# A causal convolution of matrices on one core: how the node seeds in PSUM are built, and how the stream sums are grouped

## The chip, the core and the metric

The kernel runs on one core of a Trainium2 chip. The metric is the device time of one execution in microseconds. A core has five queues that matter here: TensorE (PE in the profile; PEld are its weight loads), VectorE (DVE), ScalarE (ACT), GpSimd (POOL, which only issues loads here) and SyncE (SP, which issues stores and transposes). [...]

## The reference

`x` has shape 8 x 4096 x 512, `kernel` 8 x 512 x 512, both fp32.

```python
out = np.zeros_like(x)
for k in range(8):
    shifted = x if k == 0 else np.concatenate([zeros(B, k, D), x[:, :-k, :]], axis=1)
    out += np.matmul(shifted, kernel[k])
```

Each output row is the sum over eight matrices of the row k steps earlier times matrix k.

## The kernel before, in words

The 32768 rows are spread over 128 partitions, 256 consecutive time steps on each, and are worked through in 32 iterations of eight time steps. The eight taps are halved three times (the index letters a, b, c, each LO, HI or MID), in the manner of Karatsuba: where a plain split needs four half-size products, sums and differences of the inputs ("streams") and of the matrices leave three. So 27 products remain for an iteration in place of 64. The matrices `W[a, b, c]` are built once, ahead of the loop (lines 157 to 172), by VectorE and ScalarE, in bf16.

An iteration has three nodes, a = MID, LO and HI in this order. A node makes nine products, each of four matmuls of 128x128 by 128x512 (`product`, line 179), that is 36 matmuls a node and 108 an iteration. In the notation of the code (lines 197 to 231):

- `node_u` makes product u into bank 1 of a PSUM pair `q`; ScalarE copies it to bank 0 (line 202).
- `node_a` adds one product to each bank of q; ScalarE copies the whole pair to SBUF as `ts` (1024 elements a partition, line 209).
- `node_v`, called for b = LO and HI, makes product v into bank 1 of a pair `p`; VectorE then writes both banks of p as v + ts (LO) or v - ts (HI) in one instruction of 1024 elements, which the profile lists as pp<-pp,ts (line 215, recorded under the helper's line 79).
- `node_l` adds the last product to one bank of p; two for each p.
- `node_e` empties p: ScalarE copies it to `ms` in the MID node (line 226), VectorE adds or subtracts ms in the other two, giving y, which SP stores (lines 229 to 231).

All four pairs of banks come from one pool of four (line 54); q and p share it.

The streams are tiles in SBUF in bf16, made by VectorE from XT, which holds the eight transposed input rows: D1, D2, D21 for the MID node, D4, D41, D42, D421 for LO and HI (lines 106 to 138; all recorded under line 79, and listed as D<-XT or D<-D). A single row is 512 elements a partition. XT is filled by two transposing DMAs an iteration on SP's queue (`transpose_x`, line 100), from tiles that POOL's queue loads two iterations ahead.

The schedule is written out by hand (`manual_schedule`), and every engine works in program order. The loop of lines 239 to 272 runs over nodes; while it finishes `cur`, it begins `nxt` and makes u of the node after that. One node's order is: l and l of the first p, e of the first p, a and a of nxt with ts, first stream sums, v of nxt with its pp, twice, second stream sums, l of the second p, u of the node after next, l of the second p, e of the second p. In a LO node the first stream sums are D1, D2 and the lower half of D4, the second ones the upper half of D421, which the HI node's l products read.

Of the kernel before, what the change touches and what calls it, by code (L numbers as in the profile page):

```python
# [19 lines left out]
LO, HI, MID = 0, 1, 2  # L20
# [3 lines left out]
def kernel(  # L24
# [6 lines left out]
    nc = tc.nc  # L31
    B, S, D = x.shape
    K = kernel.shape[0]
    P = 128
# [6 lines left out]
    f32 = mybir.dt.float32  # L41
    ADD = mybir.AluOpType.add
    SUB = mybir.AluOpType.subtract
    MUL = mybir.AluOpType.mult
    PSUM = bass.MemoryType.PSUM
# [5 lines left out]
    wpool = ctx.enter_context(tc.tile_pool(name="w", bufs=1))  # L51
    spool = ctx.enter_context(tc.tile_pool(name="s", bufs=1))
    xpool = ctx.enter_context(tc.tile_pool(name="x", bufs=2))
    ppool = ctx.enter_context(tc.tile_pool(name="p", bufs=4, space=PSUM))

    ctx.enter_context(tc.manual_schedule())

# [5 lines left out]
    W = {}  # L63
# [5 lines left out]
    XT = spool.tile([P, K, D], bf, name="XT")  # L69
    D4 = spool.tile([P, K, D], bf, name="D4")  # L70
    D42 = spool.tile([P, K, D], bf, name="D42")
    D421 = spool.tile([P, K, D], bf, name="D421")
    D41 = spool.tile([P, 4, D], bf, name="D41")
    D2 = spool.tile([P, 5, D], bf, name="D2")
    D21 = spool.tile([P, 4, D], bf, name="D21")
    D1 = spool.tile([P, 2, D], bf, name="D1")

    def tt(o, a, b, op):
        nc.vector.tensor_tensor(out=o, in0=a, in1=b, op=op)  # L79


    for _ in range(4):
        pw = ppool.tile([P, 2, D], f32, name="pp")
        for h in range(2):
            nc.tensor.matmul(pw[:, h], lhsT=ident, rhs=zero, start=True, stop=True)  # L85


    def load_x(i, h):
        xin = xpool.tile([P, 4, D], bf, name="xin")
        if i >= 0:  # L90
            nc.gpsimd.dma_start(out=xin, in_=xr[:, K * i + 4 * h:K * i + 4 * h + 4, :])  # L91
        else:
            nc.vector.memset(xin, 0.0)  # L93
            for b in range(B):
                nc.gpsimd.dma_start(  # L95
                    out=xin[b * G + 1:(b + 1) * G],
                    in_=xr[b * G:(b + 1) * G - 1, RUN - 8 + 4 * h:RUN - 4 + 4 * h, :])
        return xin

    def transpose_x(xin, h):  # L100
        nc.sync.dma_start_transpose(
            out=XT[:, 4 * h:4 * h + 4, :].rearrange("p j (c m) -> p (j c) m", m=P),
            in_=xin.rearrange("p j d -> p (j d)"))


    def prep_m():
        tt(D1[:, 0], XT[:, 7], XT[:, 0], SUB)
        tt(D1[:, 1], XT[:, 0], XT[:, 1], SUB)
        tt(D2[:, 0:2], XT[:, 6:8], XT[:, 0:2], ADD)
        tt(D2[:, 2:4], XT[:, 0:2], XT[:, 2:4], ADD)  # L110

    def prep_d27():
        tt(D2[:, 4], XT[:, 5], XT[:, 7], ADD)

    def prep_d21():
        tt(D21[:, 0], D2[:, 4], D2[:, 0], SUB)
        tt(D21[:, 1:4], D2[:, 0:3], D2[:, 1:4], SUB)

    def prep_d4(h):
        a, b = (XT[:, 4:8], XT[:, 0:4]) if h == LO else (XT[:, 0:4], XT[:, 4:8])  # L120
        tt(D4[:, 4 * h:4 * h + 4], a, b, ADD)

    def prep_d41_d42(h):
        if h == LO:
            tt(D41[:, 0], D4[:, 7], D4[:, 0], SUB)
            tt(D41[:, 1], D4[:, 0], D4[:, 1], SUB)
            tt(D42[:, 0:2], D4[:, 6:8], D4[:, 0:2], ADD)
            tt(D42[:, 2:4], D4[:, 0:2], D4[:, 2:4], ADD)
        else:
            tt(D41[:, 2:4], D4[:, 3:5], D4[:, 4:6], SUB)  # L130
            tt(D42[:, 4:8], D4[:, 2:6], D4[:, 4:8], ADD)

    def prep_d421(h):
        if h == LO:
            tt(D421[:, 0], D42[:, 7], D42[:, 0], SUB)
            tt(D421[:, 1:4], D42[:, 0:3], D42[:, 1:4], SUB)
        else:
            tt(D421[:, 4:8], D42[:, 3:7], D42[:, 4:8], SUB)

# [3 lines left out]
        transpose_x(xi[h], h)  # L143
    tt(D4[:, 5:8], XT[:, 1:4], XT[:, 5:8], ADD)
    tt(D42[:, 7], D4[:, 5], D4[:, 7], ADD)
    tt(D2[:, 4], XT[:, 5], XT[:, 7], ADD)
    xi = [load_x(0, 0), load_x(0, 1)]
    transpose_x(xi[0], 0)
    prep_m()
    prep_d4(LO)  # L150
    prep_d21()
    prep_d41_d42(LO)
    transpose_x(xi[1], 1)
    prep_d4(HI)
    xi = [load_x(1, 0), load_x(1, 1)]
# [19 lines left out]
    cpool = ctx.enter_context(tc.tile_pool(name="c", bufs=2))  # L175
# [3 lines left out]
    def product(bank, comp, w, start):  # L179
        for c in range(DC):  # L180
            nc.tensor.matmul(bank, lhsT=comp[:, c * P:(c + 1) * P], rhs=w[:, c, :],  # L181
                             start=start and c == 0, stop=c == DC - 1,
                             skip_group_check=True)
# [4 lines left out]
    def streams(a):  # L188

        if a == MID:  # L190
            return (XT[:, 0], [D1[:, 0], D1[:, 1]], [D2[:, 0], D2[:, 2]],
                    [D21[:, j] for j in range(4)])
        o = 4 * a
        return (D4[:, o], [D41[:, 2 * a], D41[:, 2 * a + 1]], [D42[:, o], D42[:, o + 2]],
                [D421[:, o + j] for j in range(4)])

    def node_u(i, a):
        n = Node()
        n.i, n.a, n.s = i, a, streams(a)
        n.q = ppool.tile([P, 2, D], f32, name="pp")  # L200
        product(n.q[:, 1], n.s[0], W[a, MID, MID], True)
        nc.scalar.copy(out=n.q[:, 0], in_=n.q[:, 1])  # L202
        return n

    def node_a(n):
        product(n.q[:, 0], n.s[1][0], W[n.a, MID, LO], False)
        product(n.q[:, 1], n.s[1][1], W[n.a, MID, HI], False)
        n.ts = cpool.tile([P, 2, D], f32, name="ts")
        nc.scalar.copy(out=n.ts, in_=n.q)  # L209
        n.p = {}  # L210

    def node_v(n, b_):
        n.p[b_] = p = ppool.tile([P, 2, D], f32, name="pp")
        product(p[:, 1], n.s[2][b_], W[n.a, b_, MID], True)
        tt(p, p[:, 1:2].to_broadcast([P, 2, D]), n.ts, ADD if b_ == LO else SUB)

    ms = {}

    def node_l(n, b_, j):
        product(n.p[b_][:, j], n.s[3][2 * b_ + j], W[n.a, b_, j], False)  # L220

    def node_e(n, b_):
        p = n.p[b_]
        if n.a == MID:
            ms[b_] = mpool.tile([P, 2, D], f32, name="ms")
            nc.scalar.copy(out=ms[b_], in_=p)  # L226
        else:
            y = ypool.tile([P, 2, D], f32, name="y")
            tt(y, p, ms[b_], ADD if n.a == LO else SUB)
            t0 = K * n.i + 4 * n.a + 2 * b_  # L230
            nc.sync.dma_start(out=orr[:, t0:t0 + 2, :], in_=y)

    order = [(i, a) for i in range(NIT) for a in (MID, LO, HI)]
    nodes = [node_u(*order[0])]
    node_a(nodes[0])
    node_v(nodes[0], 0)
    node_v(nodes[0], 1)
    nodes.append(node_u(*order[1]))
    for k, (i, a) in enumerate(order):
        cur = nodes[k]  # L240
        nxt = nodes[k + 1] if k + 1 < len(order) else None
        last = i + 1 == NIT
        if a == MID and not last:
            transpose_x(xi[0], 0)
        node_l(cur, 0, LO)
        node_l(cur, 0, HI)
        node_e(cur, 0)
        if nxt:
            node_a(nxt)
        if a == MID:  # L250
            prep_d421(LO)
        elif not last and a == LO:
            prep_m()
            prep_d4(LO)
        elif not last:
            prep_d21()
            prep_d41_d42(LO)
        if nxt:
            node_v(nxt, 0)
            node_v(nxt, 1)  # L260
        if a == MID:
            prep_d41_d42(HI)
            prep_d27()
        elif a == LO:
            prep_d421(HI)
        elif not last:
            prep_d4(HI)
        node_l(cur, 1, LO)
        if k + 2 < len(order):
            nodes.append(node_u(*order[k + 2]))  # L270
        node_l(cur, 1, HI)
        node_e(cur, 1)
        if a == LO and not last:
            transpose_x(xi[1], 1)
            if i + 2 < NIT:
                xi = [load_x(i + 2, 0), load_x(i + 2, 1)]
# [30 lines left out]
```

## Time and profile before

| | us |
|---|---|
| median of 3 runs | 925.17 |
| lowest, highest | 924.97, 925.95 |
| the profiled execution | 924.67 |
| its span, first to last instruction | 922.9 |
| TensorE busy (3464 matmuls) | 758.2 |
| VectorE busy | 793.2 |
| ScalarE busy | 255.9 |
| GpSimd busy | 43.0 |

The span is what the profile shows of an execution; the rest of the execution's own time lies around it. Busy time is the union of an engine's instructions. Matmuls are pipelined, so a matmul's record is longer than the distance to the next one. The first 112 us of the span hold the input's first transposes and the building of the matrices; the loop fills the rest.

### The profile page before, as it was taken

The numbers are of one execution on the slowest core, as the hardware profiler recorded it, in microseconds if no ns is written. First come the engines' busy times: TensorE is split into PE (matmuls) and PEld (weight loads), VectorE is DVE, ScalarE is ACT, GpSimd is POOL, SyncE is SP. The second block draws the span as 40 slices with busy tenths as digits, with TensorE's granted clock in tenths as the row PEclk, the third lists the DMA queues.
The fourth block names the chain that finished last, engine by engine and source line by source line (L and its number), as shares of the span: only waits on it lengthen the run. The fifth ranks groups of instructions, "written<-read, shape, count | busy, mean of one in ns | idle before, by whom it ended". The sixth has DMA issues, their size and how long they took to land.

```text
span 922.9 us, 9305 instructions
## 1 busy us (share of the span) xinstructions
PE 758.2 (82%) x3464; PEld 336.7 (36%) x3464; DVE 793.2 (86%) x954; ACT 255.9 (28%) x329; POOL 43.0 (5%) x86
## 2 busy tenths in 40 slices
PE   1000199999999999999999999999999999999997
PEld 0000044444444444444444444444444444444443
DVE  0358679999999999999999999999999999999996
ACT  0046622222222222222222222222222222222222
POOL 4000000000000000000000000000000000000000
PEclk9999999999999999999999999999999999999999
DMA  7853317867787767677776676767677876676642
GB/s 95 116 202 130 91 40 165 181 153 174 178 173 172 158 163 179 153 161 165 182 173 157 173 180 166 155 166 177 143 172 165 181 167 166 171 182 165 155 136 114
DMA packets 169709, 145.25 MB, mean 157 GB/s; under 512 B 140752, under 2 KB 140752, under 8 KB 169664
## 3 DMA queue, kind: packets, MB, share of 16 engines
q1 hardware_dynamic: 159936, 110.12, 44.0%
q0 software_dynamic: 9728, 34.54, 23.7%
q8 instruction: 27, 0.44, 0.2%
q14 instruction: 18, 0.15, 0.1%
HBM read 77.46 MB, written 67.11 MB: 157 GB/s over the span
## 4 chain that ended last, share of the span: by engine, by line
PE 61%; DVE 21%; issue 5%; ACT 0%; DVEq 0%
PE pp L181 61%; DVE D L79 11%; DVE pp L79 7%; DVE y L79 4%; ACT ts L209 0%; DVEq L79 0%; ACT w L172 0%; ACT pp L202 0%
## 5 line engine op out<-in xcount | busy, mean ns | idle before, releaser
L181 PE MATMUL pp<-w,D 128*128 128x512 bf16 x3328 | 730.5, 380 | 61.9 <-DVE D L79 53.2
L181 PEld LDWEIGHTS <-D 128*128 128x128 bf16 x3328 | 323.2, 98 | 479.0 <-DVE D L79 69.0
L79 DVE TENSOR_TENSOR pp<-pp,ts 128x1024 f32<-128x1024 f32 x192 | 226.5, 1225 | 26.2 <-ACT ts L209 26.2
L79 DVE TENSOR_TENSOR D<-D 128x512 bf16<-128x512 bf16 (+3 forms) x353 | 239.5, 731 | 0.0
L79 DVE TENSOR_TENSOR y<-pp,ms 128x1024 f32<-128x1024 f32 x128 | 156.3, 1221 | 46.4 <-PE pp L181 46.4
L79 DVE TENSOR_TENSOR D<-XT 128x512 bf16<-128x512 bf16 (+3 forms) x226 | 152.5, 722 | 34.0 <-DMA XT<-xin 34.0
L209 ACT COPY ts<-pp 128x1024 f32<-128x1024 f32 x96 | 97.2, 1013 | 276.3 <-PE pp L181 272.8
L202 ACT COPY pp<-pp 128x512 f32<-128x512 f32 x96 | 54.7, 570 | 236.4 <-PE pp L181 236.4
L181 PE MATMUL pp<-w,XT 128*128 128x512 bf16 x128 | 34.2, 385 | 96.2 <-DVE w L79 96.2
L226 ACT COPY ms<-pp 128x1024 f32<-128x1024 f32 x64 | 64.9, 1014 | 69.5 <-PE pp L181 69.5
L91 POOL DMA_DIRECT2D xin<-in_x_dram x64 | 34.0, 531 | 827.9 <-DMA XT<-xin 827.9
L181 PEld LDWEIGHTS <-XT 128*128 128x128 bf16 x128 | 12.5, 98 | 98.5 <-issue 83.8
L79 DVE TENSOR_TENSOR mid<-wt 128x1024 f32<-128x1024 f32 (+1 forms) x12 | 18.9, 1576 | 17.2 <-DMA wt<-in_kernel_dram 17.2
L171 ACT CAST w<-mid 128x512 bf16<-128x512 f32 x20 | 12.1, 605 | 71.8 <-DVE mid L79 71.8
L79 DVE TENSOR_TENSOR w<-mid 128x512 bf16<-128x512 f32 x20 | 13.1, 689 | 0.4
L172 ACT ACTIVATE w<-mid 128x512 bf16<-128x512 f32 x20 | 12.5, 625 | 0.0
L79 DVE TENSOR_TENSOR w<-wt 128x512 bf16<-128x512 f32 x16 | 10.3, 684 | 0.0
L172 ACT ACTIVATE w<-wt 128x512 bf16<-128x512 f32 x16 | 10.0, 625 | 0.0
L171 ACT CAST w<-wt 128x512 bf16<-128x512 f32 x16 | 9.6, 602 | 0.0
L95 POOL DMA_DIRECT2D xin<-in_x_dram x16 | 8.3, 530 | 1.2 <-DVE xin L93 1.2
L79 DVE TENSOR_TENSOR mid<-mid 128x1024 f32<-128x1024 f32 x4 | 4.9, 1225 | 0.3
L85 PE MATMUL pp<-zero,ident 128*128 128x512 bf16 x8 | 3.6, 630 | 1.4 <-POOL ident masks.py:199 1.4
(10 smaller groups left out, 5.3 us busy)
## 6 DMA issues: line engine op xcount, KB each, us to landing
out_dram<-y SPq DMA_DIRECT2D x128, 512.0 KB, 3.0
xin<-in_x_dram POOLq DMA_DIRECT2D x64, 512.0 KB, 5.4
wt<-in_kernel_dram SPq DMA_DIRECT2D x8, 1024.0 KB, 4.8
XT<-xin SPq DMA_TRANSPOSE x66, 5.0
xin<-in_x_dram POOLq DMA_DIRECT2D x16, 60.0 KB, 2.6
```

What stands on the lines that cost most here:

```text
L79: nc.vector.tensor_tensor(out=o, in0=a, in1=b, op=op)
L85: nc.tensor.matmul(pw[:, h], lhsT=ident, rhs=zero, start=True, stop=True)
L91: nc.gpsimd.dma_start(out=xin, in_=xr[:, K * i + 4 * h:K * i + 4 * h + 4, :])
L95: nc.gpsimd.dma_start(out=xin[b * G + 1:(b + 1) * G], in_=xr[b * G:(b + 1) * G - 1, RUN - 8 + 4 * h:RUN - 4 + 4 * h, :])
L171: nc.scalar.copy(out=W[a, b_, LO][:, c], in_=V[:, 1])
L172: nc.scalar.mul(out=W[a, b_, HI][:, c], in_=V[:, 0], mul=-1.0)
L181: nc.tensor.matmul(bank, lhsT=comp[:, c * P:(c + 1) * P], rhs=w[:, c, :], start=start and c == 0, stop=c == DC - 1, skip_group_check=True)
L202: nc.scalar.copy(out=n.q[:, 0], in_=n.q[:, 1])
L209: nc.scalar.copy(out=n.ts, in_=n.q)
L226: nc.scalar.copy(out=ms[b_], in_=p)
```

## The change

Three things change together.

1. The seed of a node. a1 (the a product of bank 1) now comes first, into bank 1 of q; ScalarE writes its negative to bank 0. Then a0 is added to bank 0 and u to bank 1. So bank 1 holds u + a1 and bank 0 holds a0 - a1. ScalarE copies bank 1 into bank 1 of the first p, its negative into bank 1 of the second p (the seeds), and bank 0 to SBUF as `dts` (512 elements). Product v is added onto the seed in bank 1, and VectorE writes bank 0 alone, as bank 1 plus or minus dts (512 elements in place of 1024). The results are the same.
2. The pools and the order. p has three pairs of banks and q one of its own. a0 and u of nxt and the first l of the second p stand ahead of the seeds; the second l of the second p, and a1 of the node after next, behind v. D421(HI) moves ahead of v in the LO node, D4(LO) behind it; D41(HI) moves ahead of v in MID.
3. The sums. D2 is stored in another order of rows, and pairs of sums are merged into one instruction, in part through operands whose row stride is negative (`XT[:, 7::-7]` is rows 7 and 0) or larger than one.

```diff
-    ppool = ctx.enter_context(tc.tile_pool(name="p", bufs=4, space=PSUM))
+    ppool = ctx.enter_context(tc.tile_pool(name="p", bufs=3, space=PSUM))
+    qpool = ctx.enter_context(tc.tile_pool(name="q", bufs=1, space=PSUM))
...
+    def pairs(z):
+        return z.rearrange("p (a b) d -> p a (b d)", b=2)
+
     def prep_m():
-        tt(D1[:, 0], XT[:, 7], XT[:, 0], SUB)
-        tt(D1[:, 1], XT[:, 0], XT[:, 1], SUB)
-        tt(D2[:, 0:2], XT[:, 6:8], XT[:, 0:2], ADD)
-        tt(D2[:, 2:4], XT[:, 0:2], XT[:, 2:4], ADD)
+        tt(D1[:, 0:2], XT[:, 7::-7], XT[:, 0:2], SUB)
+        tt(pairs(D2[:, 1:5]), pairs(XT)[:, 3::-3], pairs(XT)[:, 0:2], ADD)
...
     def prep_d21():
-        tt(D21[:, 0], D2[:, 4], D2[:, 0], SUB)
-        tt(D21[:, 1:4], D2[:, 0:3], D2[:, 1:4], SUB)
+        tt(D21[:, 0:4], D2[:, 0:4], D2[:, 1:5], SUB)
...
-            tt(D41[:, 0], D4[:, 7], D4[:, 0], SUB)
-            tt(D41[:, 1], D4[:, 0], D4[:, 1], SUB)
-            tt(D42[:, 0:2], D4[:, 6:8], D4[:, 0:2], ADD)
-            tt(D42[:, 2:4], D4[:, 0:2], D4[:, 2:4], ADD)
+            tt(D41[:, 0:2], D4[:, 7::-7], D4[:, 0:2], SUB)
...
+            tt(pairs(D42)[:, 0:2], pairs(D4)[:, 3::-3], pairs(D4)[:, 0:2], ADD)
...
-            tt(D421[:, 0], D42[:, 7], D42[:, 0], SUB)
-            tt(D421[:, 1:4], D42[:, 0:3], D42[:, 1:4], SUB)
+            tt(D421[:, 0:4:2], D42[:, 7:0:-6], D42[:, 0:4:2], SUB)
+            tt(D421[:, 1:4:2], D42[:, 0:4:2], D42[:, 1:4:2], SUB)
...
-        n.q = ppool.tile([P, 2, D], f32, name="pp")
-        product(n.q[:, 1], n.s[0], W[a, MID, MID], True)
-        nc.scalar.copy(out=n.q[:, 0], in_=n.q[:, 1])
+        n.q = qpool.tile([P, 2, D], f32, name="qq")
+        product(n.q[:, 1], n.s[1][1], W[a, MID, HI], True)
+        nc.scalar.mul(out=n.q[:, 0], in_=n.q[:, 1], mul=-1.0)
...
+    def node_a0u(n):
         product(n.q[:, 0], n.s[1][0], W[n.a, MID, LO], False)
-        product(n.q[:, 1], n.s[1][1], W[n.a, MID, HI], False)
-        n.ts = cpool.tile([P, 2, D], f32, name="ts")
-        nc.scalar.copy(out=n.ts, in_=n.q)
+        product(n.q[:, 1], n.s[0], W[n.a, MID, MID], False)
+
+    def node_seed(n):
+        for b_ in range(2):
+            n.p[b_] = ppool.tile([P, 2, D], f32, name="pp")
+            if b_ == LO:
+                nc.scalar.copy(out=n.p[b_][:, 1], in_=n.q[:, 1])
+            else:
+                nc.scalar.mul(out=n.p[b_][:, 1], in_=n.q[:, 1], mul=-1.0)
+        n.dts = cpool.tile([P, D], f32, name="dts")
+        nc.scalar.copy(out=n.dts, in_=n.q[:, 0])

     def node_v(n, b_):
-        n.p[b_] = p = ppool.tile([P, 2, D], f32, name="pp")
-        product(p[:, 1], n.s[2][b_], W[n.a, b_, MID], True)
-        tt(p, p[:, 1:2].to_broadcast([P, 2, D]), n.ts, ADD if b_ == LO else SUB)
+        p = n.p[b_]
+        product(p[:, 1], n.s[2][b_], W[n.a, b_, MID], False)
+        tt(p[:, 0], p[:, 1], n.dts, ADD if b_ == LO else SUB)
...
         node_l(cur, 0, LO)
         node_l(cur, 0, HI)
+        if nxt:
+            node_a0u(nxt)
+        node_l(cur, 1, LO)
         node_e(cur, 0)
         if nxt:
-            node_a(nxt)
+            node_seed(nxt)
         if a == MID:
             prep_d421(LO)
-        elif not last and a == LO:
-            prep_m()
-            prep_d4(LO)
+            prep_d41(HI)
+        elif a == LO:
+            if not last:
+                prep_m()
+            prep_d421(HI)
         elif not last:
+            prep_d41(LO)
+            prep_d42(LO)
             prep_d21()
-            prep_d41_d42(LO)
         if nxt:
             node_v(nxt, 0)
             node_v(nxt, 1)
         if a == MID:
-            prep_d41_d42(HI)
+            prep_d42(HI)
             prep_d27()
-        elif a == LO:
-            prep_d421(HI)
         elif not last:
-            prep_d4(HI)
-        node_l(cur, 1, LO)
+            prep_d4(LO if a == LO else HI)
+        node_l(cur, 1, HI)
         if k + 2 < len(order):
-            nodes.append(node_u(*order[k + 2]))
-        node_l(cur, 1, HI)
+            nodes.append(node_a1(*order[k + 2]))
         node_e(cur, 1)
```

## Rows read from the trace of the kernel before

**Rows 1.** The page: busy us (share) of the engines; granted TensorE clock in 40 slices.

```profile
PE 758.2 (82%) x3464; PEld 336.7 (36%) x3464; DVE 793.2 (86%) x954; ACT 255.9 (28%) x329; POOL 43.0 (5%) x86
...
PEclk9999999999999999999999999999999999999999
```

**Rows 2.** The waits: engine and line, waited for, us in total, times, longest.

```profile
PE pp L181 <- DVE D L79: 53.2, 32, 1.7
```

**Rows 3.** Windows: one iteration; us, busy us of each engine, clock, DMA share, GB/s.

```profile
424.66:449.82 25.16, 23.48 (x109) 10.47 (x108) 23.21 (x28) 6.78 (x8) 1.06 (x2) 1.00 0.71 168
```

**Rows 4.** The timeline, a LO node into a HI node: start, us, instruction, idle before.

```profile
405.64 3.09 DVE L79 TENSOR_TENSOR D<-XT 128x512 bf16<-128x512 bf16 x5
...
408.62 1.03 PE L181 MATMUL pp<-w,XT 128*128 128x512 bf16 x4
...
408.65 2.35 DVE L79 TENSOR_TENSOR pp<-pp,ts 128x1024 f32<-128x1024 f32 x2
...
409.73 0.57 ACT L202 COPY pp<-pp 128x512 f32<-128x512 f32 x1 [2.50 <-PE pp L181]
410.91 1.21 DVE L79 TENSOR_TENSOR D<-D 128x2048 bf16<-128x2048 bf16 x1
412.05 1.22 DVE L79 TENSOR_TENSOR y<-pp,ms 128x1024 f32<-128x1024 f32 x1
...
412.18 21.76 PE L181 MATMUL pp<-w,D 128*128 128x512 bf16 x100 [1.68 <-DVE D L79]
413.72 3.24 SPq L101 DMA_TRANSPOSE XT<-xin  x1
```

**Rows 5.** Groups of instructions by shape: count, busy us, mean ns, idle before.

```profile
L79 DVE TENSOR_TENSOR pp<-pp,ts 128x1024 f32<-128x1024 f32 x192 | 226.5, 1225 | 26.2 <-ACT ts L209 26.2
...
L209 ACT COPY ts<-pp 128x1024 f32<-128x1024 f32 x96 | 97.2, 1013 | 276.3 <-PE pp L181 272.8 <-issue 3.5
L79 DVE TENSOR_TENSOR D<-D 128x2048 bf16<-128x2048 bf16 x64 | 77.8, 1216 | 0.0
...
L79 DVE TENSOR_TENSOR D<-D 128x1024 bf16<-128x1024 bf16 x96 | 63.0, 683 | 0.0
L79 DVE TENSOR_TENSOR D<-D 128x1536 bf16<-128x1536 bf16 x64 | 60.9, 951 | 0.0
L202 ACT COPY pp<-pp 128x512 f32<-128x512 f32 x96 | 54.7, 570 | 236.4 <-PE pp L181 236.4
L79 DVE TENSOR_TENSOR D<-D 128x512 bf16<-128x512 bf16 x129 | 51.1, 417 | 0.0
...
L79 DVE TENSOR_TENSOR w<-wt 128x512 bf16<-128x512 f32 x16 | 10.3, 684 | 0.0
L172 ACT ACTIVATE w<-wt 128x512 bf16<-128x512 f32 x16 | 10.0, 625 | 0.0
...
L171 ACT CAST w<-wt 128x512 bf16<-128x512 f32 x16 | 9.6, 602 | 0.0
L79 DVE TENSOR_TENSOR mid<-wt 128x2048 f32<-128x2048 f32 x4 | 9.2, 2292 | 17.2 <-DMA wt<-in_kernel_dram 17.2
```

**Rows 6.** The timeline at the loop's start: the first node's products.

```profile
111.58 0.57 ACT L202 COPY pp<-pp 128x512 f32<-128x512 f32 x1
112.21 6.39 PE L181 MATMUL pp<-w,D 128*128 128x512 bf16 x22 [8.67 <-ACT pp L202]
...
114.72 0.15 PEld L181 LDWEIGHTS <-D 128*128 128x128 bf16 x1 [0.28 <-issue]
115.15 3.17 PEld L181 LDWEIGHTS <-D 128*128 128x128 bf16 x15 [0.27 <-issue]
```

**Rows 7.** DMA issues: queue, operation, count, median us to landing.

```profile
XT<-xin SPq DMA_TRANSPOSE x66, 5.0
```

More of the change, by code (lines that the diff above doesn't have):

```diff
@@ L79, in tt @@
         nc.vector.tensor_tensor(out=o, in0=a, in1=b, op=op)
-    for _ in range(4):
-        pw = ppool.tile([P, 2, D], f32, name="pp")
+    for k in range(4):
+        pw = ppool.tile([P, 2, D], f32, name="pp") if k else qpool.tile([P, 2, D], f32, name="qq")
         for h in range(2):
@@ L103, in transpose_x @@
             in_=xin.rearrange("p j d -> p (j d)"))
+    def pairs(z):
+        return z.rearrange("p (a b) d -> p a (b d)", b=2)
     def prep_m():
-        tt(D1[:, 0], XT[:, 7], XT[:, 0], SUB)
-        tt(D1[:, 1], XT[:, 0], XT[:, 1], SUB)
-        tt(D2[:, 0:2], XT[:, 6:8], XT[:, 0:2], ADD)
-        tt(D2[:, 2:4], XT[:, 0:2], XT[:, 2:4], ADD)
+        tt(D1[:, 0:2], XT[:, 7::-7], XT[:, 0:2], SUB)
+        tt(pairs(D2[:, 1:5]), pairs(XT)[:, 3::-3], pairs(XT)[:, 0:2], ADD)
     def prep_d27():
-        tt(D2[:, 4], XT[:, 5], XT[:, 7], ADD)
+        tt(D2[:, 0], XT[:, 5], XT[:, 7], ADD)
     def prep_d21():
-        tt(D21[:, 0], D2[:, 4], D2[:, 0], SUB)
-        tt(D21[:, 1:4], D2[:, 0:3], D2[:, 1:4], SUB)
+        tt(D21[:, 0:4], D2[:, 0:4], D2[:, 1:5], SUB)
     def prep_d4(h):
@@ L121, in prep_d4, with prep_d41, prep_d42 @@
         tt(D4[:, 4 * h:4 * h + 4], a, b, ADD)
-    def prep_d41_d42(h):
+    def prep_d41(h):
         if h == LO:
-            tt(D41[:, 0], D4[:, 7], D4[:, 0], SUB)
-            tt(D41[:, 1], D4[:, 0], D4[:, 1], SUB)
-            tt(D42[:, 0:2], D4[:, 6:8], D4[:, 0:2], ADD)
-            tt(D42[:, 2:4], D4[:, 0:2], D4[:, 2:4], ADD)
+            tt(D41[:, 0:2], D4[:, 7::-7], D4[:, 0:2], SUB)
         else:
             tt(D41[:, 2:4], D4[:, 3:5], D4[:, 4:6], SUB)
+    def prep_d42(h):
+        if h == LO:
+            tt(pairs(D42)[:, 0:2], pairs(D4)[:, 3::-3], pairs(D4)[:, 0:2], ADD)
+        else:
             tt(D42[:, 4:8], D4[:, 2:6], D4[:, 4:8], ADD)
@@ L145 @@
     tt(D42[:, 7], D4[:, 5], D4[:, 7], ADD)
-    tt(D2[:, 4], XT[:, 5], XT[:, 7], ADD)
+    prep_d27()
     xi = [load_x(0, 0), load_x(0, 1)]
@@ L190, in streams @@
         if a == MID:
-            return (XT[:, 0], [D1[:, 0], D1[:, 1]], [D2[:, 0], D2[:, 2]],
+            return (XT[:, 0], [D1[:, 0], D1[:, 1]], [D2[:, 1], D2[:, 3]],
                     [D21[:, j] for j in range(4)])
@@ L195, in streams, with node_a1 @@
                 [D421[:, o + j] for j in range(4)])
-    def node_u(i, a):
+    def node_a1(i, a):
         n = Node()
         n.i, n.a, n.s = i, a, streams(a)
-        n.q = ppool.tile([P, 2, D], f32, name="pp")
-        product(n.q[:, 1], n.s[0], W[a, MID, MID], True)
-        nc.scalar.copy(out=n.q[:, 0], in_=n.q[:, 1])
+        n.q = qpool.tile([P, 2, D], f32, name="qq")
+        product(n.q[:, 1], n.s[1][1], W[a, MID, HI], True)
+        nc.scalar.mul(out=n.q[:, 0], in_=n.q[:, 1], mul=-1.0)
+        n.p = {}
         return n
-    def node_a(n):
+    def node_a0u(n):
         product(n.q[:, 0], n.s[1][0], W[n.a, MID, LO], False)
-        product(n.q[:, 1], n.s[1][1], W[n.a, MID, HI], False)
-        n.ts = cpool.tile([P, 2, D], f32, name="ts")
-        nc.scalar.copy(out=n.ts, in_=n.q)
-        n.p = {}
+        product(n.q[:, 1], n.s[0], W[n.a, MID, MID], False)
[4 more added lines that the diff above has]
+                nc.scalar.copy(out=n.p[b_][:, 1], in_=n.q[:, 1])
+            else:
+                nc.scalar.mul(out=n.p[b_][:, 1], in_=n.q[:, 1], mul=-1.0)
+        n.dts = cpool.tile([P, D], f32, name="dts")
+        nc.scalar.copy(out=n.dts, in_=n.q[:, 0])
     def node_v(n, b_):
-        n.p[b_] = p = ppool.tile([P, 2, D], f32, name="pp")
-        product(p[:, 1], n.s[2][b_], W[n.a, b_, MID], True)
-        tt(p, p[:, 1:2].to_broadcast([P, 2, D]), n.ts, ADD if b_ == LO else SUB)
+        p = n.p[b_]
+        product(p[:, 1], n.s[2][b_], W[n.a, b_, MID], False)
+        tt(p[:, 0], p[:, 1], n.dts, ADD if b_ == LO else SUB)
     ms = {}
@@ L233 @@
     order = [(i, a) for i in range(NIT) for a in (MID, LO, HI)]
-    nodes = [node_u(*order[0])]
-    node_a(nodes[0])
+    nodes = [node_a1(*order[0])]
+    node_a0u(nodes[0])
+    node_seed(nodes[0])
     node_v(nodes[0], 0)
     node_v(nodes[0], 1)
-    nodes.append(node_u(*order[1]))
+    nodes.append(node_a1(*order[1]))
     for k, (i, a) in enumerate(order):
@@ L246 @@
         node_l(cur, 0, HI)
+        if nxt:
+            node_a0u(nxt)
+        node_l(cur, 1, LO)
         node_e(cur, 0)
         if nxt:
-            node_a(nxt)
+            node_seed(nxt)
         if a == MID:
             prep_d421(LO)
-        elif not last and a == LO:
-            prep_m()
-            prep_d4(LO)
+            prep_d41(HI)
[3 more added lines that the diff above has]
+            prep_d421(HI)
         elif not last:
+            prep_d41(LO)
+            prep_d42(LO)
             prep_d21()
-            prep_d41_d42(LO)
         if nxt:
```

## The prediction

> **What bounds the kernel now.** I read the busy shares first: VectorE 86%, TensorE 82%, ScalarE 28%, and TensorE's granted clock at nine tenths or more in every slice [rows 1]. Two engines near full and neither full points at their coupling, so next comes the list of waits for TensorE: past the weight preparation it waits for one thing, 32 times, 1.7 us at most, 53.2 us in all: VectorE's stream sums [rows 2]. One iteration (three nodes, 108 matmuls) takes 25.16 us by the windows and holds 23.48 us of TensorE work and 23.21 us of VectorE work [rows 3]. The timeline shows the place [rows 4]. A LO node's VectorE queue runs without a gap: y, five sums from XT, two pp, the D421 sum of the HI node (128x2048, 410.91), y. TensorE has finished its last product of the node and stands until that sum ends at 412.12; it starts again at 412.18. The sum stands behind two pp of 1.22 us each.
>
> TensorE's own pace: 100 matmuls take 21.76 us and 4 take 1.03 us [rows 4], so starts are (21.76 - 1.03) / 96 = 0.216 us apart, a product of four is 0.864 us, a node of nine is 7.77 us, an iteration 23.32 us. A matmul's record lasts 1.03 - 3 x 0.216 = 0.38 us, 0.16 more than its slot, so each wait of 1.68 us is a hole of 1.84 us: 23.32 + 1.84 = 25.16, the iteration measured. All holes: 53.2 + 32 x 0.16 = 58.4 us.
>
> **The change, part by part.** Time t counts from the start of a node's first product; all products are those of before, in another order: l, l, a0, u, l, v, v, l, a1.
>
> *VectorE.* The six pp of an iteration fall from 1024 to 512 elements. The rows have 1.225 us for 1024 and 2.292 for 2048 fp32 elements, so 0.69 for 512, which the 512-element sums from wt (0.684) confirm [rows 5]: 6 x 0.535 = 3.2 us less. Merged sums: two 512 (0.417 each) become one 1024 (0.683) for D1 and D41, two 1024 one 2048 (1.216) for D2 and D42, 512 + 1536 (0.417 + 0.951) one 2048 for D21, and two 1024 for D421, which saves nothing [rows 5]. Back to back an instruction overlaps the next by 0.09 us (two pp take 2.35 [rows 4]), so a merge saves about 0.07: 0.35 us an iteration. VectorE's work becomes 23.2 - 3.5 = 19.7 us, under TensorE's 23.3.
>
> But the queue is in order, so I walk it, each duration less 0.09. LO node: l to bank 1 ends at 0.864 + 1.03 = 1.89, y starts at 1.93; D1 3.06, D2 3.66, D421(HI) 4.79, the two pp 5.92 and 6.52, D4(LO) 7.12, second y 8.25, free 9.4. v's product for the first pp ends at 5 x 0.864 + 1.03 = 5.35, so it is there in time. That pp ends at 6.61; TensorE needs it at 7.77. D421(HI) now ends at 6.0, needed at 7.77: the old hole is gone, with 1.2 us to spare at the next-latest thing, the pp. HI node: VectorE is free at 9.4 - 7.77 = 1.63, before its y can start, and the same queue lengths follow (D41, D42, D21 in front of the pp). MID node: no y, about 4.5 us of sums, idle for the rest. So VectorE never ends last. Removed: 58.4 us.
>
> *ScalarE.* Per node the ts copy (1.013) goes; two seeds and dts of 512 elements come. The 512-element copy between PSUM banks is 0.570; a mul costs 0.02 more than a copy (0.625 against 0.602) [rows 5]. dts to SBUF lies between 0.57 and the 0.60 of the casts. That is 1.75 us for 1.01, three times an iteration: ScalarE goes from some 28% to 38%, not a bound. What matters is a new hand-over in TensorE's path: u, first seed, v. u's last matmul ends at 3 x 0.864 + 1.03 = 3.62. ScalarE's copy of before starts 0.08 after the product it waits for (408.62 + 1.03, then 409.73 [rows 4]); after a ScalarE copy TensorE starts 0.06 later (111.58 + 0.57, then 112.21 [rows 6]). So v can start at 3.62 + 0.08 + 0.57 + 0.06 = 4.33; its slot is 5 x 0.864 = 4.32. One product, the l put between u and v, covers the seed almost exactly. Bounds: nothing (hand-overs a little shorter), or 0.1 us with one more semaphore to take first. I take 0.02 a node, the rows' sum and some restart: 96 x 0.02 = 2 us. Behind the waiting v in TensorE's queue stand the rest of the node and the next one, so a delay here is a delay of everything. The second seed ends 0.5 us after the first, v's second product a product later; dts ends at 5.3, when pp's turn is 5.92. [...]
>
> *Buffers.* Three pp buffers and one q replace four pp. A node's second seed takes the buffer that the current node's first bank pair leaves: y starts at 1.93 and ends at 3.15, the MID copy (about as long as ts) at 3.0; the seed wants it at 4.2. Were it late, dts would queue behind it on ScalarE, and pp on VectorE behind dts. q is free for a1 (slot 6.91) when dts ends at 5.3. The mul behind a1 (ends 8.6) is wanted by a0 at 7.77 + 1.73 = 9.5. All cost nothing, with 1 us or more in hand; without that cover each would stall TensorE once a node.
>
> *Transposes.* D4(LO) moves behind the pp, but the second transpose was queued on SP behind the second y's store and still is. It starts 0.45 us after that y ends (413.27, 413.72 [rows 4]) and lands 5.0 us later [rows 7]: HI node t = 9.5 - 7.77 + 0.45 + 5.0 = 7.2, while D4(HI) has its turn at 7.12. VectorE may wait 0.1 us there, in front of a y that nothing waits for. The first transpose, behind HI's second y, lands at t = 7.2 of MID, 3.6 us before D1. Nothing on POOL's queue moves but with these landings. The DMA share of 0.71 in an iteration [rows 3] becomes 0.71 x 25.16 / 23.4 = 0.76, no bound.
>
> *Ahead of the loop.* The first node has no l to cover its seed: after u, v starts 0.08 + 0.57 + 0.06 later, where before it followed at once: some 0.9 us with the drain of u's last matmul. TensorE's first weight loads there still start 0.43 apart (114.72, 115.15 [rows 6]), half the later pace; should the gap keep it slow for v, four matmuls cost 0.85 more. I take 0.9, with 1.8 as the upper bound. The merged D1 and D2 stand in front of a transpose and the weight loads: 0.1 us less. The tail keeps its order: nothing.
>
> **Sum.** The profiled execution took 924.67 us (span 922.9); it stands 0.5 under the median 925.17. 924.67 - 58.4 + 2 + 0.9 - 0.1 = 869.1. Against the median 869.5; I say 869. By the bounds: 866 without any hand-over cost, 878 with 0.1 a node and the slow start.
>
> **Rivals.**
>
> *The hand-over is longer.* ScalarE takes several semaphores in front of a seed, and each 0.1 us costs 96 x 0.1 = 9.6 us: 876 for 0.1 with the usual start, 886 for 0.2. For: the slack is 0.01 us. Against: each piece has a row. Chance 0.12.
>
> *Operands of negative row stride lose the double rate.* bf16 sums take 1.216 us for 2048 elements where fp32 ones take 2.292 [rows 5]; no row has a negative stride. At the fp32 pace D1, D41 and one D421 sum gain 0.54 us each, D2 and D42 1.08. In LO the first pp then ends at 6.61 + 1.62 = 8.23, TensorE starts at 8.29: 0.52 lost. VectorE enters HI at 9.4 + 1.62 - 8.29 = 2.73, 0.8 late; its pp ends 6.61 + 1.62 + 0.8 = 9.03, 1.32 lost; MID absorbs the rest. Together 1.84 an iteration, just what the old hole cost; with the 2 us of hand-overs, 0.9 ahead of the loop and 1.5 on the sums before the weight loads the kernel would take about 929. Against: within a row the stride stays one. [...] Chance 0.05.
>
> *Slower: v waits for the whole seeding.* If TensorE's wait for the first seed is released only by dts, the last of the three, v starts at 3.62 + 0.08 + 0.57 + 0.50 + 0.50 + 0.06 = 5.33, 1.01 late, in every node: 96 x 1.01 = 97 us against 58 removed, 964. It decides from 0.61 us a node on. Against: ScalarE's copy starts 0.08 us after its product while TensorE runs on [rows 4], so waits here are counted by single instructions. Chance 0.03.
>
> **How the numbers follow.** Forecast 0.77, longer hand-over 0.12, lost rate 0.05, whole seeding 0.03, unseen causes 0.03. The range 865 to 886 takes the forecast with its bounds and the longer hand-over. Runs lie within 0.1%, so 0.2% is about what can be told from no change. Faster by more than that: the first two and most of the unseen, 0.91; slower: the other two, less the part of the lost rate that ends at the old time, 0.06; same 0.03.
>
> **What would show it.** Right: iterations of 23.3 to 23.4 us; TensorE's wait for the D sums gone, in its place at most hundredths of a microsecond for ScalarE's pp; VectorE's pp at 0.69 us with 512 elements and busy some 19.7 us an iteration; the merged sums at 0.68 and 1.22 us. Wrong: seeds well over 0.57 us, TensorE waits for ScalarE pp of over 0.1 us, sums at 1.2 and 2.3 us, or a granted clock below full now that TensorE has no hole.

## The result, and the profile after

The changed kernel takes 868.33 us (median of 4 runs, 864.72 to 868.93), the kernel before 925.07 in the same comparison: a ratio of 0.938, 95% interval 0.935 to 0.941. 869.0 was forecast, in 865 to 886. The profiled execution took 864.72 us, its span 862.9.

The page after, busy time and granted clock, against [rows 1]:

```profile
PE 753.3 (87%) x3464; PEld 339.3 (39%) x3464; DVE 686.6 (80%) x794; ACT 308.5 (36%) x521; POOL 42.8 (5%) x86
...
PEclk6555589999999999999999999999999999999999
```

TensorE has the same 3464 matmuls in 60 us less, VectorE 160 instructions fewer. The clock row reads lower ahead of the loop, where TensorE is nearly idle: the granted clock is 0.54 in the first 107.9 us, in which TensorE is busy for 5.8 us, 0.86 from there to 129.4 us, and 1.00 behind that. That gives this profile its mean granted clock of 0.938, against 0.999 before. It is no difference of the kernels: other runs of the kernel before read 0.94 too (926.44 us) as well as 1.00 (923.15 us), and in its profile the first weight loads also started 0.43 us apart [rows 6], although no lower clock was recorded there (1.00 over the first 112.2 us).

Windows of the changed kernel, one iteration (columns as in [rows 3]):

```profile
454.50:477.82 23.32, 23.32 (x110) 10.54 (x109) 19.88 (x24) 8.42 (x15) 1.05 (x2) 1.00 0.77 179
```

An iteration is now 23.32 us long and TensorE is busy in all of it; VectorE has 19.88 us of work in place of 23.21. The waits after, the same view as [rows 2]; the first three rows are all that TensorE's matmuls have past the first eight (line 86, at 1.4 to 4.8 us), and lie ahead of the loop:

```profile
PE qq L186 <- ACT w L177: 94.2, 4, 51.6
...
PE qq L186 <- ACT qq L210: 8.2, 1, 8.2
...
PE pp L186 <- ACT pp L222: 0.7, 1, 0.7
...
DVE pp L80 <- ACT dts L226: 46.9, 28, 1.8
```

The row for the D sums, 53.2 us in 32 waits, is gone; the one wait for a seed belongs to the first node. The last row is VectorE's, waiting for dts; it does so in MID nodes, where it has time.

The groups by shape after, against [rows 5]:

```profile
L80 DVE TENSOR_TENSOR D<-D 128x2048 bf16<-128x2048 bf16 x128 | 153.3, 1218 | 0.0
L80 DVE TENSOR_TENSOR pp<-pp,dts 128x512 f32<-128x512 f32 x192 | 127.6, 694 | 62.8 <-ACT dts L226 46.9 <-PE pp L186 12.1
L80 DVE TENSOR_TENSOR D<-XT 128x2048 bf16<-128x2048 bf16 x96 | 117.0, 1220 | 11.4 <-DMA XT<-xin 9.8 <-DVE pp L80 0.4
...
L226 ACT COPY dts<-qq 128x512 f32<-128x512 f32 x96 | 58.2, 606 | 0.0
L224 ACT ACTIVATE pp<-qq 128x512 f32<-128x512 f32 x96 | 56.6, 590 | 0.0
L210 ACT ACTIVATE qq<-qq 128x512 f32<-128x512 f32 x96 | 55.9, 582 | 263.9 <-PE qq L186 263.9
L222 ACT COPY pp<-qq 128x512 f32<-128x512 f32 x96 | 54.7, 570 | 175.6 <-PE qq L186 170.3 <-DVE D L80 3.6 <-DVE y L80 1.7
...
L80 DVE TENSOR_TENSOR D<-XT 128x1024 bf16<-128x1024 bf16 x32 | 21.8, 682 | 6.9 <-DMA XT<-xin 6.9
```

pp takes 0.694 us. All 32 sums D<-XT of 1024 elements are D1, whose first operand has a negative row stride: 0.682 us, as the plain ones before (0.683). A third of the 96 of 2048 elements are D2, also negative; the mean of the 96 is 1.220, that of the 32 D2 alone 1.218, against 1.216 before. So a negative row stride costs nothing here.

The timeline of a LO node into a HI node after, the place of [rows 4] (TensorE and ScalarE at the seeds, VectorE's queue):

```profile
453.66 1.82 DVE L80 TENSOR_TENSOR D<-XT 128x1024 bf16<-128x1024 bf16 x2
...
454.04 3.63 PE L186 MATMUL pp<-w,D 128*128 128x512 bf16 x16
...
454.30 0.57 ACT L222 COPY pp<-qq 128x512 f32<-128x512 f32 x1 [1.94 <-PE qq L186]
454.78 0.59 ACT L224 ACTIVATE pp<-qq 128x512 f32<-128x512 f32 x1
455.27 0.61 ACT L226 COPY dts<-qq 128x512 f32<-128x512 f32 x1
455.39 1.22 DVE L80 TENSOR_TENSOR D<-D 128x2048 bf16<-128x2048 bf16 x1
456.53 1.29 DVE L80 TENSOR_TENSOR pp<-pp,dts 128x512 f32<-128x512 f32 x2
...
457.73 1.22 DVE L80 TENSOR_TENSOR D<-XT 128x2048 bf16<-128x2048 bf16 x1
...
458.37 1.89 PE L186 MATMUL pp<-w,D 128*128 128x512 bf16 x8
...
458.86 1.22 DVE L80 TENSOR_TENSOR y<-pp,ms 128x1024 f32<-128x1024 f32 x1
...
460.30 1.22 DVE L80 TENSOR_TENSOR y<-pp,ms 128x1024 f32<-128x1024 f32 x1 [0.22 <-PE pp L186]
```

D421 for the HI node stands ahead of the pp and ends at 456.61; the first pp ends at 457.22. TensorE begins the HI node at 458.37, 1.15 us later, as walked. The second product of the 16-matmul stretch, v, is due 0.86 us after 454.04, at 454.90; the seed ends at 454.87, and v begins at 454.92. So the hand-over is 0.01 us late, in LO nodes alone. There the copy to the first seed starts 0.06 us later than in the other two (0.092 us behind u's last matmul, against a median of 0.037). In the trace it takes two semaphores in turn, VectorE's or its own and the product's (the first two copies of the kernel wait for the product's alone); in LO nodes the product's is taken first (at 454.24 above, in 17 ns), and the other one comes after it.

### The profile page after: what moved, and what is told of

It reads as the page before. It is cut to its first block, busy times and chain, and to the rows that moved or that the text cites. A ratio compares the mean times of both kernels' runs of the same rounds, so it can differ in the third digit from the quotient of the medians.

```text
span 862.9 us, 9334 instructions
## 1 busy us (share of the span) xinstructions
PE 753.3 (87%) x3464; PEld 339.3 (39%) x3464; DVE 686.6 (80%) x794; ACT 308.5 (36%) x521; POOL 42.8 (5%) x86
## 3 DMA queue, kind: packets, MB, share of 16 engines
q0 software_dynamic: 9728, 34.54, 25.8%
## 4 chain that ended last, share of the span: by engine, by line
PE 87%; DMA 5%; ACT 3%; DVE 3%; POOL 1%; issue 0%; SPq 0%; DVEq 0%
PE pp L186 58%; PE qq L186 29%; DMA wt<-in_kernel_dram 3%; DMA XT<-xin 2%; ACT w L177 2%; DVE mid L80 2%; ACT w L176 2%; POOL xin L96 1%; DVE D L80 1%; DMA xin<-in_x_dram 1%; DVE y L80 0%; DVE xin L94 0%; ACT pp L222 0%; SPq L167 0%; ACT qq L210 0%
## 5 line engine op out<-in xcount | busy, mean ns | idle before, releaser
L186 PE MATMUL pp<-w,D 128*128 128x512 bf16 x2304 | 529.0, 379 | 0.7 <-ACT pp L222 0.7
L186 PE MATMUL qq<-w,D 128*128 128x512 bf16 x1024 | 254.5, 381 | 102.4 <-ACT w L177 94.2
L80 DVE TENSOR_TENSOR D<-D 128x2048 bf16<-128x2048 bf16 (+2 forms) x257 | 233.1, 948 | 0.0
L80 DVE TENSOR_TENSOR D<-XT 128x2048 bf16<-128x2048 bf16 (+3 forms) x162 | 150.9, 948 | 41.3 <-DMA XT<-xin 39.7
L80 DVE TENSOR_TENSOR pp<-pp,dts 128x512 f32<-128x512 f32 x192 | 127.6, 694 | 62.8 <-ACT dts L226 46.9
L210 ACT ACTIVATE qq<-qq 128x512 f32<-128x512 f32 x96 | 55.9, 582 | 263.9 <-PE qq L186 263.9
L222 ACT COPY pp<-qq 128x512 f32<-128x512 f32 x96 | 54.7, 570 | 175.6 <-PE qq L186 170.3
L226 ACT COPY dts<-qq 128x512 f32<-128x512 f32 x96 | 58.2, 606 | 0.0
L224 ACT ACTIVATE pp<-qq 128x512 f32<-128x512 f32 x96 | 56.6, 590 | 0.0
L186 PE MATMUL qq<-w,XT 128*128 128x512 bf16 x128 | 33.7, 387 | 0.0
```

The lines of the kernel that those rows point to most:

```text
L210: nc.scalar.mul(out=n.q[:, 0], in_=n.q[:, 1], mul=-1.0)
L222: nc.scalar.copy(out=n.p[b_][:, 1], in_=n.q[:, 1])
L224: nc.scalar.mul(out=n.p[b_][:, 1], in_=n.q[:, 1], mul=-1.0)
L226: nc.scalar.copy(out=n.dts, in_=n.q[:, 0])
```

## The experiments

The theory under test: TensorE's pace bounds the loop, and what it loses is set by where D421 and the pp stand in VectorE's queue, and by the one product that covers the first seed. The main rival: the time follows VectorE's total work, which the change cut by 3.3 us an iteration. Medians are set against the kernel before on the same chip (ratio and 95% interval), because the time ahead of the loop scatters by some microseconds from profile to profile (107.7 to 114.2 us with the old opening).

**The order alone.** The seeds, the 1024-element pp and the separate sums of before, in the new order:

```diff
         node_l(cur, 0, HI)
+        if nxt:
+            node_a(nxt)
+        node_l(cur, 1, LO)
         node_e(cur, 0)
         if nxt:
-            node_a(nxt)
+            node_ts(nxt)
...
-        elif not last and a == LO:
-            prep_m()
-            prep_d4(LO)
+        elif a == LO:
+            if not last:
+                prep_m()
+            prep_d421(HI)
```

(`node_ts` is the copy to ts, split off from `node_a`; the other moves are those of the change.)

> The seeds, the pp of 1024 elements and the separate sums of the kernel before, in the new order. Theory (the hole was D421's place in VectorE's queue; TensorE bounds everything else): walking VectorE's queue, the LO node's first pp ends at 7.25 us of 7.77, but its second y ends late, so HI's queue starts 0.85 late and its first pp ends at 8.16: a hole of 0.45 us an iteration in place of 1.84, so 925.1 - 32 x 1.39 = 881 us (876 to 886). Rival (the time follows VectorE's work): that work stays at 23.2 us an iteration, so 915 to 925 us.

Measured: 885.5 us, ratio 0.957 (0.952 to 0.962). The timeline, a HI node's start:

```profile
400.40 14.84 PE L189 MATMUL pp<-w,D 128*128 128x512 bf16 x67 [0.39 <-DVE pp L79]
...
424.26 5.99 PE L189 MATMUL pp<-w,D 128*128 128x512 bf16 x26 [0.39 <-DVE pp L79]
```

Iterations of 23.86 us, with one hole of 0.39 + 0.16 = 0.55 us where 0.45 was walked, and it is the pp that now comes last, as the theory has it. VectorE's work is that of before, so the rival falls: the order without any lighter work brings over two thirds of the gain.

**The order and the merged sums.** As above with the change's sums:

```diff
-        tt(D1[:, 0], XT[:, 7], XT[:, 0], SUB)
-        tt(D1[:, 1], XT[:, 0], XT[:, 1], SUB)
+        tt(D1[:, 0:2], XT[:, 7::-7], XT[:, 0:2], SUB)
...
```

> As the run with the order alone, and with the merged sums; seeds and pp of 1024 elements still those of before. Theory: HI's first pp ends at 7.87, a hole of 0.16 us an iteration, 871 us (867 to 875): nearly the whole gain with no change in the seeds. Rival (the time follows VectorE's work): 0.35 us an iteration less work than before, 914 us (910 to 920).

Measured: 876.85 us, ratio 0.948 (0.943 to 0.953), above the forecast of 867 to 875. Most iterations are as walked: from y to y 23.52 us, a hole of 0.20.

```profile
742.22 1.23 DVE L79 TENSOR_TENSOR y<-pp,ms 128x1024 f32<-128x1024 f32 x1 [0.42 <-PE pp L185]
...
765.74 1.22 DVE L79 TENSOR_TENSOR y<-pp,ms 128x1024 f32<-128x1024 f32 x1 [0.42 <-PE pp L185]
```

But five lose 0.3 to 1.3 us, 4.2 us together, each behind a late transpose in front of D1 (timeline of one of them):

```profile
199.19 1.83 DVE L79 TENSOR_TENSOR D<-XT 128x1024 bf16<-128x1024 bf16 x2 [0.91 <-DMA XT<-xin]
...
203.35 7.93 PE L185 MATMUL pp<-w,D 128*128 128x512 bf16 x35 [0.29 <-DVE pp L79]
...
211.89 1.46 PE L185 MATMUL pp<-w,D 128*128 128x512 bf16 x6 [0.60 <-DVE pp L79]
```

VectorE waits 0.91 us for XT in front of D1, and TensorE then loses 0.45 and 0.76 us in the two nodes behind. With 22.8 us of VectorE work in an iteration of 23.5 us there is next to no slack to take that up. In the changed kernel VectorE met longer waits of the same kind (timelines of VectorE's queue at two of them):

```profile
490.80 1.22 DVE L80 TENSOR_TENSOR D<-XT 128x2048 bf16<-128x2048 bf16 x1 [1.88 <-DMA XT<-xin]
...
794.06 1.23 DVE L80 TENSOR_TENSOR D<-XT 128x2048 bf16<-128x2048 bf16 x1 [1.90 <-DMA XT<-xin]
```

and TensorE lost 0.1 us behind each of these two. Part of the difference is the place: here it is D4 that waits, behind the pp. So what the lighter seeds themselves bring is the last 0.2 us an iteration and the slack for late transposes; the next kernel shows a wait in front of D1 with the light seeds.

**The sums apart.** The changed kernel with the separate sums of before (the reverse of the diff above).

> The changed kernel with all sums separate again, as they were before. Theory: the first pp comes 0.14 to 0.2 us later, with over 1 us in hand, so nothing: 868.3 us (867 to 870), iterations of 23.32 us. Rival (the time follows VectorE's work): 0.35 us an iteration more, 879 us.

Measured: 863.78 us (862.91 to 869.34), below the forecast of 867 to 870; ratio 0.936 (0.932 to 0.940), against 0.938 with the merged sums. The loop is not what is shorter. VectorE's first pp of two LO nodes in a row:

```profile
456.42 1.29 DVE L80 TENSOR_TENSOR pp<-pp,dts 128x512 f32<-128x512 f32 x2
...
479.73 1.29 DVE L80 TENSOR_TENSOR pp<-pp,dts 128x512 f32<-128x512 f32 x2
```

They are 23.31 us apart: the loop is the same. This kernel also met a late transpose in front of D1, as the kernel with the order and the merged sums did (timeline there, D1 and the HI node's start):

```profile
500.88 1.97 DVE L80 TENSOR_TENSOR D<-XT 128x512 bf16<-128x512 bf16 x4 [0.60 <-DMA XT<-xin]
...
504.91 1.89 PE L191 MATMUL pp<-w,D 128*128 128x512 bf16 x8
```

VectorE waits 0.60 us, and TensorE goes into the HI node without a wait. So in the same place, with the light seeds, such a wait is taken up. The merged sums bring nothing to the changed kernel; they count only where the queue in front of a late sum is full.

**The merged sums alone**, in the kernel before.

> The kernel before with the merged sums alone; order and seeds as before. Theory (only what stands in front of D421 in the LO node's queue counts): D1 and D2 merged start D421 0.14 us earlier, the hole shrinks from 1.84 to 1.70 us an iteration, 4.5 us: ratio 0.995. Rival (the time follows VectorE's work): 0.35 us an iteration, 11 us: ratio 0.988.

Measured: 920.81 us, ratio 0.996 (0.994 to 0.999), which holds the theory's 0.995 and not the rival's 0.988. The timeline at the old hole:

```profile
411.14 1.22 DVE L79 TENSOR_TENSOR D<-D 128x2048 bf16<-128x2048 bf16 x1
...
412.41 15.93 PE L188 MATMUL pp<-w,D 128*128 128x512 bf16 x71 [1.54 <-DVE D L79]
```

1.54 + 0.16 = 1.70 us a hole, 0.14 less than before: only D1 and D2, which stand in front of D421, count, and the other merges vanish in VectorE's idle time.

**D421 late.** The changed kernel with two sums exchanged:

```diff
             if not last:
                 prep_m()
-            prep_d421(HI)
+                prep_d4(LO)
...
-        elif not last:
-            prep_d4(LO if a == LO else HI)
+        elif a == LO:
+            prep_d421(HI)
+        elif not last:
+            prep_d4(HI)
```

> The changed kernel with D421 of the HI node behind the two pp of the LO node again and the lower half of D4 in front of them; VectorE's work is the same. Theory (its place in the queue is what counts): D421 starts at 7.11 and ends at 8.33 us of the LO node, TensorE starts the HI node at 8.39 in place of 7.77: a hole of 0.62 us an iteration, 868.3 + 20 = 888 us (884 to 892), with TensorE's wait for the D sums back 32 times. Rival (the time follows VectorE's work): 868 us.

Measured: 885.27 us, ratio 0.959 (0.954 to 0.964). The timeline:

```profile
418.02 1.22 DVE L80 TENSOR_TENSOR D<-D 128x2048 bf16<-128x2048 bf16 x1
...
419.29 1.90 PE L186 MATMUL pp<-w,D 128*128 128x512 bf16 x8 [0.69 <-DVE D L80]
```

TensorE stands until D421 ends at 419.24, though the two pp in front of it are short now. A matmul is missing from the records ahead of this wait, so the hole is 0.69 - 0.22 + 0.16 = 0.63 us, where 0.62 was walked. Same work, other place, 2% of the time.

**No cover.** The changed kernel with the l between u and v moved behind v:

```diff
             node_a0u(nxt)
-        node_l(cur, 1, LO)
         node_e(cur, 0)
...
+        node_l(cur, 1, LO)
         node_l(cur, 1, HI)
```

> The changed kernel with the first l of the second p moved from between u and v to behind v; nothing else. Theory (that product is what covers the hand-over u, ScalarE's seed, v): v is due 0.86 us earlier, at 3.46 us of the node, and can start at 3.62 + 0.04 + 0.57 + 0.05 = 4.28, so TensorE waits 0.83 us in each of 96 nodes, 0.06 more in the LO ones: 868.3 + 81 = 949 us (940 to 957), slower than the kernel before. Rival (the seeds lie beside TensorE's path): 868 us.

Measured: 943.17 us, ratio 1.021 (1.017 to 1.026): slower than the kernel before. TensorE's rows of three nodes, each at v:

```profile
399.67 3.61 PE L186 MATMUL pp<-w,D 128*128 128x512 bf16 x16 [0.87 <-ACT pp L222]
...
408.26 3.61 PE L186 MATMUL pp<-w,D 128*128 128x512 bf16 x15 [0.66 <-ACT pp L222]
...
416.90 0.38 PE L186 MATMUL pp<-w,D 128*128 128x512 bf16 x1 [0.71 <-ACT pp L222]
```

0.66 + 0.16 = 0.82 us in MID and HI nodes, 0.71 + 0.16 = 0.87 in LO nodes. (The 0.87 of the first row has a matmul missing from the records in front of it.) The seeds are on TensorE's path, and one product hides them.

**dts first.** The changed kernel with ScalarE's copy to dts ahead of the two seeds:

```diff
     def node_seed(n):
+        n.dts = cpool.tile([P, D], f32, name="dts")
+        nc.scalar.copy(out=n.dts, in_=n.q[:, 0])
         for b_ in range(2):
...
-        n.dts = cpool.tile([P, D], f32, name="dts")
-        nc.scalar.copy(out=n.dts, in_=n.q[:, 0])
```

> The changed kernel with the copy to dts issued ahead of the two seeds on ScalarE; nothing else. Theory (the first seed has next to no slack): the first seed ends 0.50 us later, v starts at 4.78 in place of 4.32, 0.47 us lost in MID and HI nodes and 0.53 in LO nodes: 868.3 + 47 = 915 us (908 to 920). Rival (the seeds lie beside TensorE's path, or have the slack that dts has): 868 us.

Measured: 912.88 us, ratio 0.987 (0.982 to 0.991). The timeline of one hand-over:

```profile
404.15 0.58 ACT L220 COPY dts<-qq 128x512 f32<-128x512 f32 x1 [1.88 <-PE qq L186]
404.63 0.59 ACT L224 COPY pp<-qq 128x512 f32<-128x512 f32 x1
405.14 0.57 ACT L226 ACTIVATE pp<-qq 128x512 f32<-128x512 f32 x1
405.27 2.75 PE L186 MATMUL pp<-w,D 128*128 128x512 bf16 x12 [0.30 <-ACT pp L224]
```

v starts 0.05 us after the first seed ends (405.22) and not after the second (405.71), 0.30 + 0.16 = 0.46 us late. It is 0.46 in LO nodes too, where 0.53 was forecast. It also answers the rival that v might wait for the whole seeding: TensorE's waits are released by single instructions.

**Weights first.** The holes are gone, so what remains besides 746 us of matmuls is the time ahead of the loop. This version queues the first loads of the kernel tensor on SP ahead of the transposes and puts the input's first sums between the four chunks of matrices:

```diff
     with tc.tile_pool(name="wt", bufs=1) as tp:
+        h0, h1, g0 = w_load(tp, 0, 0), w_load(tp, 0, 1), w_load(tp, 1, 0)
+        xi = [load_x(-1, 0), load_x(-1, 1)]
+        for h in range(2):
+            transpose_x(xi[h], h)
+        w_make(tp, 0, [h0, h1])
+        h0, h1, g0 = g0, w_load(tp, 1, 1), w_load(tp, 2, 0)
...
+        transpose_x(xi[0], 0)
+        w_make(tp, 1, [h0, h1])
...
```

(`w_load` and `w_make` are the body of the old loop over chunks.)

> The changed kernel with the building of the matrices ahead: the first three loads of the kernel tensor are queued on SP ahead of the transposes, and the input's first stream sums stand between the four chunks of matrices in VectorE's queue. Theory (with no hole left in the loop, what remains is the 109 us ahead of it): four chunks of 12 to 14 us from some 11 us on and 8 us of stream sums between them let the first a0 start at 70 to 78 us, the loop is unchanged: 868.3 - 35 = 833 us (828 to 842). Rival (the transposes, 8 to 43 us and one behind the other, set the start): 850 to 865 us.

Measured: 833.81 us (833.40 to 834.49), ratio 0.902 (0.898 to 0.906). The timeline, SP's first issue and TensorE's first a0:

```profile
0.74 1.55 SPq L147 DMA_DIRECT2D wt<-in_kernel_dram  x3
...
78.53 1.87 PE L194 MATMUL qq<-w,D 128*128 128x512 bf16 x4 [8.21 <-ACT qq L218]
```

The timeline of the changed kernel at the same a0, the u behind it and the first v:

```profile
109.53 1.86 PE L186 MATMUL qq<-w,D 128*128 128x512 bf16 x4 [8.21 <-ACT qq L210]
...
111.19 1.91 PE L186 MATMUL qq<-w,XT 128*128 128x512 bf16 x4
...
113.75 1.89 PE L186 MATMUL pp<-w,D 128*128 128x512 bf16 x8 [0.66 <-ACT pp L222]
```

The a0 starts 31.0 us earlier, half a microsecond past the 70 to 78 that were forecast. From there to the end the two profiled executions take 755.4 and 755.2 us: the loop is unchanged. Both kernels are beaten, and the four runs lie within 1.1 us, where those of the others scatter by 4 to 9.

## Why the prediction was right

By its own steps:

- *The old hole.* 58.4 us were to go, and the wait for the D sums went whole. The walk of VectorE's queue held: D421 ended 1.76 us ahead of TensorE's need and the pp 1.15, where 1.77 and 1.16 were walked. The order alone and D421 late show that the place in the queue does it, by 1.29 us an iteration without lighter work and 0.63 with it.
- *VectorE's work.* 19.7 us an iteration were forecast, 19.88 came; pp 0.694 for 0.69; the merged sums kept their rate, so the rival of the lost rate is out by the rows. What they save, 0.35 us an iteration, brought nothing, as their 1 us of slack said it would.
- *The hand-over.* 2 us for 96 nodes was the mis-sized term: it measured about 0.01 us in 32 LO nodes, 0.4 us in all. The row of before had 0.08 us between a product and ScalarE's copy; that row includes a second semaphore, taken after the product's, and where the product's comes last the copy starts 0.04 us after the product. The path itself was as described: taking its cover away cost 0.82 us a node, putting 0.5 us in it 0.46. The seeds lasted what the rows of before had given: the copy 570 ns, the mul 590.
- *The first node.* v followed u's last start by 1.29 us (113.75, after u from 111.19 on) where 0.43 is the pace there: 0.86 us for 0.9. TensorE came out of that gap at full pace (the eight matmuls from 113.75 take 1.89 us), so the 0.85 us more of the bound did not come.
- *Transposes.* D4(HI) was to wait 0.1 us; in ten iterations VectorE waited longer there, up to 1.9 us. The forecast took the median landing, and the second transpose, which D4(HI) waits for, kept it (5.03 us before, 5.04 after, when the two transposes of an iteration are taken apart in the trace). But single ones land later, up to 6.7 us before and 6.9 after, and with its turn right at the median D4(HI) now meets each of them; before, its turn came at 420.61 us in the stretch of [rows 4], 1.9 us behind such a landing (413.72 + 5.0). It stands where TensorE loses at most 0.1 us by it, 0.2 us in all.
- *The sum.* For the profiled execution 924.67 - 58.8 (the holes by the starts of matmuls) + 0.9 + 0.4 gives 867.2, and 864.72 was measured. The rest is 2.5 us. The 0.2 us behind D4(HI) go the other way, and 2.7 us lie ahead of the loop: the first product behind ScalarE's copy started at 109.53 against 112.21 [rows 6]. From there to the end the two profiled executions take 812.5 and 755.2 us, 57.3 less, which is 58.8 - 0.9 - 0.4 - 0.2. VectorE's first sum waited 25.8 us for XT before and 23.1 after (groups by shape of the two kernels):

```profile
L79 DVE TENSOR_TENSOR D<-XT 128x1536 bf16<-128x1536 bf16 x1 | 1.0, 958 | 25.8 <-DMA XT<-xin 25.8
...
L80 DVE TENSOR_TENSOR D<-XT 128x1536 bf16<-128x1536 bf16 x1 | 1.0, 959 | 23.1 <-DMA XT<-xin 23.1
```

Across the profiles of all kernels with the old opening that start lies between 107.7 and 114.2 us, so this is scatter and not the change, and that the median comes within 0.7 us of the forecast is in part luck: the loop itself came out 1.8 us shorter than forecast, 1.6 of it the hand-over. The prediction also took runs to lie within 0.1%, from three of them; thirteen later runs of the kernel before spread from 919.16 to 927.21 us, 0.9%.

Against the rival of the lost rate the prediction had that the stride within a row stays one; that this leaves the sums fast was the author's expectation, with no row of before behind it. The 0.682 us of D1 shows it for a negative step between rows. A negative step within a row is not shown here.

## What to carry to other kernels

When two engines are both near full, do not compare their totals: walk the in-order queue of the one and ask, for each thing that the other needs, what stands in front of it. The new order, D421 ahead of the two pp above all, brought about two thirds of this gain without any lighter work; exchanging that one sum again in the changed kernel costs 2%. The lighter instructions brought the rest, and the slack that keeps it when a transfer is late. A hand-over through another engine is free only while something of its length stands between; here one product of 0.86 us covers 0.82 (and falls 0.01 short of the 0.87 in LO nodes), and that margin is to be counted before it is used.

## What was not expected

- The seed's margin is a few hundredths of a microsecond, and the order in which a ScalarE copy takes its two semaphores (0.06 us) decides whether it holds: LO nodes lose 0.013 us at v, MID and HI nodes nothing.
- The transposes land later: a median of 6.2 us in place of 5.0 [rows 7]. The rows of the pages of the changed kernel and of the one without cover:

```profile
XT<-xin SPq DMA_TRANSPOSE x66, 6.2
...
XT<-xin SPq DMA_TRANSPOSE x66, 5.8
```

It is not the faster loop that does it: without cover an iteration takes 25.82 us, longer than before, and the median is up all the same. It is the first of the two transposes alone, from 5.2 us to 6.0 or more, in every kernel with the new order; the kernel before with the merged sums alone stays at 5.0. What in the order does it is not shown.

- The scatter of several microseconds between profiles lies ahead of the loop. From the first a0 on, the three kernels with the same loop (the changed one, the one with the sums apart and the one with the weights first) take 755.2, 755.9 and 755.4 us, while with the old opening the a0 itself starts anywhere from 107.7 to 114.2 us. With the weights first the four runs lie within 1.1 us. That the runs of one kernel scatter for the same reason is likely but not shown, since each kernel left one profile.
